# Keys of the cached sequences turned in place in three whole rooms, with the closing work of a sequence one period later and the sliding keys turned ahead of the scores

## The chip, the cores and the metric

The kernel runs on one core of one Trainium2 chip. The metric is the time of one execution on the device in microseconds (us), the median of several runs. Five engines work side by side, each through its own list of instructions in order: PE (TensorE: matmuls, and 128x128 transposes as matmuls with an identity), DVE (VectorE), ACT (ScalarE), POOL (GpSimd) and SP (SyncE, which here only issues transfers). POOL issues transfers too. An instruction that waits holds up all that stands behind it on its engine.

## The reference

The reference is one step of a one-layer decoder trunk. Two branches of attention are projected, merged by gates, and followed by an MLP. There are two groups of tokens: a prompt of 512 tokens, and a sample of 8 sequences with 8 new tokens each. Each sequence of the sample also has 2048 cached tokens, which lie in 16 pages of 128 tokens anywhere in a pool; a page table says where.

```
def fox_attend(q, cq, q_pos, k, v, ck, k_pos):
    s = jnp.einsum('btgrd,bsgd->bgrts', q, k).astype(jnp.float32) * HEAD_DIM ** -0.5
    bias = jnp.moveaxis(cq, 1, -1)[..., :, None] - jnp.moveaxis(ck, 1, -1)[..., None, :]
    p = masked_softmax(s + bias, k_pos[None, :] <= q_pos[:, None])
    return jnp.einsum('bgrts,bsgd->btgrd', p.astype(v.dtype), v)
...
    nsa_all = jnp.concatenate([gather_pages(nsa_pool, page_table), pm['nsa_rows']], axis=1)
    kc, vc, c_end = compressed_kv(nsa_all[:, :, 0], nsa_all[:, :, 1], lp)
...
    win_all = jnp.concatenate([win_buf, pm['win_rows']], axis=1)
...
    o_nsa = nsa_attend(pm['nsa_q'], pos[past:], pm['nsa_gate'], kc, vc, c_end, ks_blk, vs_blk,
                       win_all[:, :, 0], win_all[:, :, 1], w_pos)
```

For this case the attention of the sample over its cache matters. Each sequence has 64 rows of queries for the forgetting branch (8 heads by 8 tokens) and 64 for the sparse branch. Both meet all 2048 cached keys of the sequence (the sparse branch with a mask of chosen blocks added), a softmax follows, and the weights meet the 2048 cached values. The sparse branch has beside this a sliding window of 512 keys per sequence, and compressed keys, which an earlier stage has finished. All arithmetic here is in float32.

## The kernel before, in words

The stages are: conditioning and projections; attention of the prompt; attention of the sample (`sample_attention`); gates and branch projections (`mix_part`); output projection; MLP. A scheduler with a model of the engines sets the order inside most stages. Inside the sample's attention the order of PE's work is the one in which the code is written (`self.chain`).

**A sequence's data.** The cached rows of a sequence are 4.2 MB: 2 MB of the forgetting branch (`foxD`, gathered earlier into one place) and 2 MB of the sparse branch, page by page from `cache_nsa_kv`. They are loaded in four quarters (`sample_load`). A quarter is one transfer of 512 KB and four of 128 KB, one kind issued by SP and the other by POOL (line 155), by turns. The quarters go round a ring of ten places, called `r2`, `rp`, `L`, `s` and `U` in the code, with two quarters each; so two and a half sequences have room. In the trace the tiles are named `rows` (the places `r2` and `rp`), `fr` and `sr`. A row holds 128 numbers of keys and 128 of values.

**A sequence's period.** For sequence b the steps are:

1. `key_turn` (L1646): eight transposes on DVE in blocks of 32x32, from the quarters into two tiles `KT`. A ninth (L1650, `CT`) turns the bias terms, which POOL copies first (L1648).
2. `sequence_scores`: 64 matmuls `ss<-KT` and 8 `ss<-CT` on PE, each with 512 columns into a bank of its quarter. DVE adds a ramp and takes the maximum (L1671, `sS`), four times.
3. `new_scores` (`sn`, L1682): the scores against the new tokens.
4. `sequence_weights`: maximum over all (L1688, L1689 on DVE), then three exponentials on ACT.
5. `turn_weights`: 16 PE transposes `sp` and their eviction by ACT (`spT`), and one `spn` (`TN`).
6. `values(b)`: 128 + 4 matmuls `so<-rows`, `so<-fr`, `so<-sr`, `so<-vnew`. They are done one period later, behind the scores of b+1.
7. `sequence_end` (L1728 and on, `OA`) and `sums` (`accS`): scaling and the sum over heads, right behind `values`.

The window works for two sequences at once. On even b, behind the scores and values, come `window_keys` (`wk`, eight PE transposes), `window_scores` (`sw`, L1756) and `window_weights`. On odd b come `window_turned` (`spw`, `spwn`, evicted into `TW` by ACT and DVE) and `window_values` (`so<-wr`, `so<-vnew,TW`, `so<-vc`), then the loads of the next two windows (`wr`).

**The order of a period before.** Scores of b; new scores; weights of b; on odd b the window's values and loads; values of b-1; closing of b-1; the four quarters 4b+6 to 4b+9, that is the last two of b+1 and the first two of b+2; on even b the sums of two sequences; `key_turn` of b+1 (held back until the maximum of b is taken); on even b the window's keys, scores and weights; the turning of the weights of b. In the last period the first matmuls of the gates (`mix_first`, `mg<-hH`) stand ahead of the last `turn_weights`; their weights (`wmr`, `wmh`) are loaded from the last exponential on, and `hL` takes the place `r2` after the last values.

Helpers: L77 is every matmul, L83 every PE transpose, L112 every ACT operation, L115 a copy, L104 and L106 operations with a scalar, L155 a transfer.

## Time and profile before

| | |
|---|---|
| median of 3 runs | 1332.19 us (1330.32 to 1332.41) |
| the profiled execution, its own time | 1332.86 us |
| its span, first to last instruction | 1331.2 us |
| mean granted TensorE clock | 0.936 |
| PE busy | 1220.8 us (92%) |
| DVE busy | 689.3 us (52%) |
| ACT busy | 495.6 us (37%) |
| POOL busy | 179.6 us (13%) |

The last eviction of the prompt's attention starts at 465.6 us, the copies of the sample's result at 687.3 and 687.6 us; the sample's attention lies between. A line of the profile that groups instructions gives the engine, the operation, output and inputs by the program's names, shapes and count, then the busy time and the mean of one, then the idle time of the engine ahead of them and what ended it. A line of the waits gives the engine and the instruction that waited, what it waited for, then the total, the number of waits and the longest. A line of the windows gives a stretch of time, its length, the busy time of PE, of its weight loads, of DVE, ACT and POOL (with numbers of instructions), then the granted clock (1.00 is full speed), the DMA engines' mean busy share and the GB/s that they moved.

### The profile page before, as it was taken

The numbers are of one execution on the slowest core, as the hardware profiler recorded it, in microseconds if no ns is written. First come the engines' busy times: TensorE is split into PE (matmuls) and PEld (weight loads), VectorE is DVE, ScalarE is ACT, GpSimd is POOL, SyncE is SP. The second block draws the span as 40 slices with busy tenths as digits, with TensorE's granted clock in tenths as the row PEclk, the third lists the DMA queues.
The fourth block names the chain that finished last, engine by engine and source line by source line (L and its number), as shares of the span: only waits on it lengthen the run. The fifth ranks groups of instructions, "written<-read, shape, count | busy, mean of one in ns | idle before, by whom it ended". The sixth has DMA issues, their size and how long they took to land. (4 is left out here: it accounts for less than half of the span.)

```text
span 1331.2 us, 24902 instructions
## 1 busy us (share of the span) xinstructions
PE 1220.8 (92%) x9561; PEld 1018.3 (76%) x9561; DVE 689.3 (52%) x1820; ACT 495.6 (37%) x1082; POOL 179.6 (13%) x252
## 2 busy tenths in 40 slices
PE   4899989998999986687868999999999999999998
PEld 4777879996666533433468999999899898898996
DVE  4687756685788453433333434465334343343445
ACT  3444444445777621321332223346432142231321
POOL 2101000003213122312120000000111020111110
PEclk9899989999999966866678999999999999999999
DMA  8785266877756354654464333403342142232202
GB/s 229 227 252 163 91 206 205 268 259 229 246 180 189 112 183 162 227 184 159 135 161 141 85 82 103 127 1 96 95 127 67 60 121 70 64 95 83 76 17 71
DMA packets 164057, 188.11 MB, mean 141 GB/s; under 512 B 16186, under 2 KB 141571, under 8 KB 161763
## 3 DMA queue, kind: packets, MB, share of 16 engines
q1 hardware_dynamic: 145218, 146.15, 36.1%
q0 software_dynamic: 13408, 37.23, 8.6%
q10 hardware_dynamic: 5312, 3.15, 0.9%
q8 instruction: 75, 1.23, 0.4%
q14 instruction: 44, 0.35, 0.1%
HBM read 176.48 MB, written 30.90 MB: 156 GB/s over the span
## 5 line engine op out<-in xcount | busy, mean ns | idle before, releaser
L1984 POOL TENSOR_TENSOR u<-u 128x576 f32<-128x576 f32 x32 | 53.9, 1685 | 417.7 <-ACT u L112 327.7
L77 PE MATMUL mg<-hH,wmh 128*128 128x288 f32 x256 | 77.2, 303 | 7.2 <-ACT wmh L112 7.2
L77 PE MATMUL mg<-hL,wmh 128*128 128x288 f32 x256 | 74.8, 303 | 6.7 <-DMA hL<-hfd 6.7
L100 DVE TENSOR_TENSOR acc<-acc,dn 128x512 f32<-128x512 f32 x60 | 39.8, 686 | 77.4 <-PE dn L77 77.4
L77 PE MATMUL ss<-KT,scr 32*32 32x512 f32 x512 | 54.8, 932 | 26.6 <-DVE KT L1646 26.6
L77 PE MATMUL mg<-hH,wml 128*128 128x288 f32 x256 | 77.2, 303 | 0.7 <-DVE wml L131 0.7
L112 ACT ACTIVATE xh<-ct 128x256 fp32r<-128x256 f32 x128 | 48.0, 384 | 59.9 <-PE ct L83 38.4
L131 DVE TENSOR_TENSOR xl<-ct,xh 128x256 fp32r<-128x256 f32 x128 | 51.5, 421 | 17.6 <-ACT xh L112 15.8
L83 PE MATMUL ct<-identF,ro 128*128 128x128 f32 x256 | 37.7, 289 | 24.6 <-DVE ro L115 18.9
L763 DVE TENSOR_TENSOR u<-u,u 128x512 fp32r<-128x512 f32 x64 | 28.3, 484 | 61.3 <-ACT u L112 61.3
L131 DVE TENSOR_TENSOR wml<-wmr,wmh 128x1024 fp32r<-128x1024 f32 x16 | 19.6, 1225 | 76.3 <-ACT wmh L112 76.3
L77 PE MATMUL z<-winh,h2r 128*128 128x264 f32 (+1 forms) x288 | 57.1, 288 | 0.0
L77 PEld LDWEIGHTS ss<-KT,scr 32*32 32x32 f32 x512 | 12.5, 139 | 56.8 <-issue 47.7
L77 PE MATMUL z<-winh,h 128*128 128x264 f32 (+1 forms) x288 | 55.7, 283 | 0.0
L77 PEld LDWEIGHTS mg<-hH,wmh 128*128 128x128 f32 x256 | 49.9, 195 | 7.3 <-ACT wmh L112 7.3
L77 PEld LDWEIGHTS mg<-hL,wmh 128*128 128x128 f32 x256 | 48.1, 193 | 8.0 <-DMA hL<-hfd 8.0
L1671 DVE CUSTOM_DVE_ANT_1 sS<-ss,scr 128x512 f32<-128x512 f32 x32 | 20.8, 689 | 63.6 <-PE ss L77 63.6
L83 PEld LDWEIGHTS ct<-identF,ro 128*128 128x128 f32 x256 | 30.8, 150 | 28.1 <-DVE ro L115 17.5
L77 PEld LDWEIGHTS mg<-hH,wml 128*128 128x128 f32 x256 | 49.8, 195 | 1.0 <-DVE wml L131 1.0
L77 PEld LDWEIGHTS z<-winh,h2r 128*128 128x128 f32 x288 | 45.5, 189 | 1.2 <-issue 0.8
L77 PEld LDWEIGHTS z<-winh,h 128*128 128x128 f32 x288 | 45.7, 189 | 0.0
L112 ACT ACTIVATE u<-up 128x256 f32<-128x256 f32 (+1 forms) x96 | 27.8, 324 | 48.1 <-PE up L77 48.0
(849 smaller groups left out, 3670.3 us busy)
## 6 DMA issues: line engine op xcount, KB each, us to landing
adw<-in_w_ada SPq DMA_DIRECT2D x16, 1024.0 KB
foxD<-in_cache_fox_kv SPq DMA_DIRECT2D x128, 128.0 KB
wur<-in_w_up SPq DMA_DIRECT2D x32, 512.0 KB
wdr<-in_w_down SPq DMA_DIRECT2D x32, 512.0 KB
cpg<-in_cache_nsa_kv SPq DMA_DIRECT2D x120, 128.0 KB
wada<-in_w_ada POOLq DMA_DIRECT2D x8, 1024.0 KB, 6.9
wmr<-in_w_in SPq DMA_DIRECT2D x16, 512.0 KB
winr<-in_w_in SPq DMA_DIRECT2D x10, 512.0 KB
```

The source lines that it names most:

```text
L77: ins = self.nc.tensor.matmul(out, a, b, start=start, stop=stop, skip_group_check=True)
L83: ins = self.nc.tensor.transpose(out, in_, self.identF[:n, :n])
L100: self.nc.vector.tensor_tensor(out, a, b, op=op)
L112: return self.nc.scalar.activation(out, in_, f, **kw)
L131: self.splits.append((eng or self.nc.vector).tensor_tensor(l, x, h.bitcast(F32), op=OP.subtract).ins)
L763: (eng or self.nc.vector).tensor_tensor(h2[:, o:o + n], x[:, i:i + n], h2[:, i:i + n].bitcast(F32), op=OP.subtract)
L1671: self.nc.vector.tensor_tensor_reduce(self.S[:, :, q, :], pbs[q].rearrange("p (c s) -> p c s", s=32), self.ramp[:, None, 32 * (q % 2):32 * ...
L1984: nc.gpsimd.tensor_tensor(u[j], u[j], u[j], op=OP.mult)
```

## The change: three rooms, keys turned in place, another order of the period

**Rooms.** A sequence now has a room of its own for all 16 pages, and there are three: sequence b takes room b mod 3. Room 0 is made of the places `r2` (forgetting branch) and `rp` (sparse branch), rooms 1 and 2 lie in pools of their own. The load keeps its four quarters of transfers. Sequence 0 is loaded during the prompt's attention; 1 and 2 at the start of the sample's attention, behind the first two windows; b+2 in the period of b, behind the values of b-1, which free the room.

**Keys.** The eight transposes write back to where they read. The tiles `KT` are gone. The scores' matmuls read their 512 columns as 16 runs of 32 numbers, one run per page, 1 KB apart; before, the 512 numbers lay side by side.

**Order of a period.** On even b the window's keys come ahead of the scores, its scores behind the new scores, its weights behind the maximum. On odd b the window's turning and values (`window_back`) come ahead of the values of b-1. The closing of b-2 now stands in period b, behind the maximum; the sums come at the end of odd periods, one pair later. `key_turn` of b+1 follows the closing. The second part of `TW` is evicted by ACT.

**End.** In the last period the window's values, the values of sequence 6, the load of `hH` and the opening of the gates' weights come ahead of the last scores. The first gate matmuls stand between the last turning, values and closings.

The core of the diff:

```diff
             if n == 8:
                 self.forget_load(pn)
-                with self.tc.issue_after(self.last_min):
-                    for u in (2, 3):
-                        self.sample_load(u)
...
             if n == 9:
                 assert not (self.ada_open or self.ada_next)
-                for u in range(2):
-                    self.sample_load(u)
+                with self.tc.issue_after(self.last_min):
+                    self.sample_load(0)
...
-    RING = ("r2", "r2", "rp", "rp", "L", "L", "s", "s", "U", "U")
...
+        k = b % 3
+        if k == 0:
+            f = self.keep.tile([P, 16, 256], F32, tag="r2", bufs=1, name=f"fr{b}")
+            r = self.rp.tile([P, 16, 256], F32, tag="rp", name=f"sr{b}")
         else:
...
+            f, r = [self.spools[k].tile([P, 16, 256], F32, tag=n, bufs=1, name=f"{n}{b}") for n in ("fr", "sr")]
+        for i in range(4):
+            one, two = ("gpsimd", "sync") if i % 2 else ("sync", "gpsimd")
+            self.dma(two, f[:, 4 * i:4 * i + 4], self.foxD[b][:, 4 * i:4 * i + 4])
...
-        for u in range(4, 10):
-            self.sample_load(u)
-            if u == 5:
-                for b in range(2):
-                    self.window_load(b)
         self.key_turn(sp, 0)
+        for b in range(2):
+            self.window_load(b)
+        self.sample_load(1)
+        self.sample_load(2)
         self.sample_maps(sp)
...
+            if b == last:
+                self.window_back(pw, n)
                 self.values(b - 1)
...
+                self.hH = self.rp.tile([P, NK, NT], F32R, tag="rp", name="hH")
+                self.dma("gpsimd", self.hH, self.hfd[:, :, 0:NT])
+                ctx.close()
+                self.mix_open()
+            if not odd:
                 for o in range(2):
...
+                    self.window_keys(pw, b + o)
+            self.sequence_scores(sp, b)
+            self.new_scores(sp, b)
+            if not odd:
+                self.window_scores(pw, n)
+            self.sequence_max(b)
+            if not odd:
+                self.window_weights(n)
+            if b > 1:
+                self.sequence_end(sp, b - 2)
+                if not odd:
+                    self.window_end(sp, n - 1)
+            if b < last:
                 with self.tc.issue_after(self.last_stat):
                     self.key_turn(sp, b + 1)
-            if on and not odd:
+            if odd and b < last:
+                self.window_back(pw, n)
                 for o in range(2):
...
+                    self.window_load(b + 1 + o)
+            if 0 < b < last:
+                self.values(b - 1)
+                if b + 2 < NB:
+                    self.sample_load(b + 2)
+            self.turn_weights(sp, b)
+            if odd and b > 1:
+                self.pair_sums(n - 1)
+        self.mix_first(0)
+        self.values(last)
+        self.window_end(sp, 3)
+        for k in (1, 2):
+            self.mix_first(k)
+        for b in (last - 1, last):
+            self.sequence_end(sp, b)
+        self.mix_first(3)
+        self.pair_sums(3)
...
-        self.KT = [sp.tile([P, 4, 16, 32], F32, tag=f"KT{n}", bufs=1, name=f"KT{n}_{b}") for n in range(2)]
         for i in range(4):
-            for n, src in enumerate(self.rows[4 * b + i]):
-                self.nc.vector.transpose(self.KT[n][:, :, 4 * i:4 * i + 4, :].rearrange("p k c s -> p c k s"),
-                                         src[:, :, 0:P].rearrange("p c (k d) -> p c k d", k=4))
+            for src in self.rows[b]:
+                v = src[:, 4 * i:4 * i + 4, 0:P].rearrange("p c (k d) -> p c k d", k=4)
+                self.nc.vector.transpose(v, v)
...
-                                self.KT[x // 2][part[q], 2 * (x % 2) + e].rearrange("p c s -> p (c s)"), e == 0, False)
+                                self.rows[b][x // 2][part[q], :, 64 * (x % 2) + 32 * e:64 * (x % 2) + 32 * e + 32], e == 0, False)
...
-        self.cp(self.TW[:NS, 4], tn[:NS, 0:P])
+        self.act(self.TW[:NS, 4], tn[:NS, 0:P])
```

The scheduler places the transposes of sequence 0 on DVE. This is DVE's list before, in the last part of the prompt's attention (`Sfox` adds a bias to the prompt's scores and takes a maximum, `oT<-ofox` evicts an output):

```order
L104 TENSOR_SCALAR ncn<-cumn 64x64 [waits PE_49]
L115 COPY scr<-scr 64x8x8 [waits DVE_49]
L115 COPY scr<-scr 64x4x8 x2
L104 TENSOR_SCALAR scr<-scr 128x64 [waits DVE_49]
L100 TENSOR_TENSOR oT<-ofox_6095,Ffox_6069 128x512 [waits PE_49,Activation_49]
L100 TENSOR_TENSOR scr<-pers,scr 128x8x64 [waits DVE_49]
L1203 ISA Sfox_6181,nmfox_6182<-sfox_6203,browfox_5911 128x512 [waits PE_49]
```

And now, at the same place:

```order
L104 TENSOR_SCALAR ncn<-cumn 64x64 [waits PE_49]
L100 TENSOR_TENSOR scr<-pers,scr 128x8x64 [waits DVE_49]
L1652 STREAM_TRANSPOSE fr_6121<-fr_6121 128x4x128 [waits DMAHW4_49,DMASW0_49]
L1652 STREAM_TRANSPOSE sr_6122<-sr_6122 128x4x128 [waits DMAHW6_49,DMAHW7_49,DMAHW1_49,DMAHW0_49]
L100 TENSOR_TENSOR oT<-ofox_6065,Ffox_6039 128x512 [waits PE_49,Activation_49]
L1200 ISA Sfox_6182,nmfox_6183<-sfox_6221,browfox_5913 128x128 [waits PE_49]
L1200 ISA nmfox_6183 128x1
L1652 STREAM_TRANSPOSE fr_6121<-fr_6121 128x4x128 [waits DMAHW2_49]
```

The first transposes of the sample, each waiting for its transfers, now stand ahead of an output's eviction and of the maxima of the prompt's scores; before, the first of them stood behind the last `oT<-ofox`.

POOL's list at the start of the sample's attention, before (`jj` is a ramp of 64 numbers from which DVE makes the selectors `sel` and `selW`; an `ISA` computes a page's address):

```order
L1216 COPY ffox_6419<-denfox_6352 128x512
L155 DMA fr_6533<-foxD_80 128x1024
L162 TENSOR_LOAD ptp
L155 ISA
L155 DMA sr_6550<-in_cache_nsa_kv 128x256
...
L155 DMA wr_6565<-in_state_win_kv 128x1024
L155 DMA wr_6567<-in_state_win_kv 128x1024
L155 DMA fr_6569<-foxD_80 128x1024
L125 IOTA jj 128x64
```

And now:

```order
L1213 COPY ffox_6418<-denfox_6351 128x512
L155 DMA wr_6543<-in_state_win_kv 128x1024
L155 DMA wr_6545<-in_state_win_kv 128x1024
L155 DMA fr_6547<-foxD_80 128x1024
...
L155 DMA fr_6605<-foxD_81 128x1024
L162 TENSOR_LOAD ptp
L155 ISA
L155 DMA sr_6606<-in_cache_nsa_kv 128x256
...
L155 DMA sr_6606<-in_cache_nsa_kv 128x256
L125 IOTA jj 128x64
```

The ramp stood behind POOL's share of two quarters, both windows and one transfer more; now it stands behind both windows and POOL's whole share of sequences 1 and 2, 22 transfers. On DVE the first selector, which waits for the ramp, stood ahead of all four `sS` of sequence 0; now it stands between the second and the third.

ACT's list in an odd period, before (`sS` and `sN` are the exponentials of the sequence, `spT` evicts its turned weights):

```order
L112 ACTIVATE TW_7971<-spw_7964 128x512
L112 ACTIVATE sS_7949,ss_5_7947<-sS_7949,ss_5_7948 128x1024 x2
L112 ACTIVATE sN_7957,ss_5_7947<-sN_7957,ss_5_7948 128x64
L112 ACTIVATE spT_8161<-sp_8156 128x512
L112 ACTIVATE spT_8168<-sp_8163 128x512
```

And now:

```order
L112 ACTIVATE TW_7969<-spw_7962 128x512
L112 ACTIVATE sS_7931,ss_5_7929<-sS_7931,ss_5_7930 128x1024 x2
L112 ACTIVATE sN_7939,ss_5_7929<-sN_7939,ss_5_7930 128x64
L112 ACTIVATE TW_7969<-spwn_7963 64x128
L112 ACTIVATE spT_8131<-sp_8126 128x512
```

The eviction of `spwn`, for which PE's `so<-vnew,TW` waits, came from DVE; now it stands on ACT behind the three exponentials.

More of the change, by code (lines that the diff above doesn't have):

```diff
@@ L1406, in sample_select @@
         pb = self.accb("selx")
[L1407 removed]
+        sel2 = self.carve([P, 2, 32])
         nc.vector.memset(sel2, 0.0)
@@ L1571, in sample_attention @@
         self.key_turn(sp, 0)
+        for b in range(2):
+            self.window_load(b)
+        self.sample_load(1)
+        self.sample_load(2)
         self.sample_maps(sp)
-        for b in range(NB + 1):
-            n, odd, on = b // 2, b % 2, b < NB
-            if on:
-                self.sequence_scores(sp, b)
-                self.new_scores(sp, b)
-                self.sequence_weights(b)
-            if on and odd:
-                self.window_turned(pw, n)
-                self.window_values(sp, n)
-                if b + 2 < NB:
-                    for o in range(2):
-                        self.window_load(b + 1 + o)
-            if b:
-                self.values(b - 1)
-                self.sequence_end(sp, b - 1)
-                for u in range(4 * b + 6, min(4 * b + 10, 4 * NB)):
-                    self.sample_load(u)
-            if on and odd:
-                self.window_end(sp, n)
-            if b and not odd:
-                for o in range(2):
-                    self.sums(b - 2 + o, self.sel, self.OA[o], True)
-                    self.sums(b - 2 + o, self.selW[o], self.OAw, False)
-            if b + 1 < NB:
+        last = NB - 1
@@ new lines, in sample_attention @@
+        for b in range(NB):
+            n, odd = b // 2, b % 2
+            if b == last:
+                self.window_back(pw, n)
+                self.values(b - 1)
+                self.hH = self.rp.tile([P, NK, NT], F32R, tag="rp", name="hH")
[3 more added lines that the diff above has]
+            if not odd:
+                for o in range(2):
+                    self.window_keys(pw, b + o)
[11 more added lines that the diff above has]
+            if b < last:
@@ L1617, in sample_attention, with window_back, pair_sums @@
             self.cp(self.oT[:, 4 * a:4 * a + 4, SEQ:NT].rearrange("p r (b t) -> p r b t", t=8), av[:, a])
+    def window_back(self, pw, n):
+        self.window_turned(pw, n)
+        self.window_values(pw, n)
+    def pair_sums(self, n):
+        w = self.OAw.pop(n)
+        for o in range(2):
+            self.sums(2 * n + o, self.sel, self.OA.pop(2 * n + o), True)
+            self.sums(2 * n + o, self.selW[o], w, False)
     def sample_maps(self, sp):
@@ L2050, in run @@
         self.staged = 0
-        self.rows, self.wr, self.pair = {}, {}, {}
+        self.rows, self.wr, self.wst = {}, {}, {}
         actx = ExitStack()
```

71 lines of the change are left out of this document (23 added, 48 removed).

## The prediction

> **What bounds the kernel now.** I read the page first. PE is busy for 92% of the span; the rows of the forty slices (33.3 us each, tenths) tell where it is not, and where its clock is low:
>
> ```profile
> PE   4899989998999986687868999999999999999998
> PEclk9899989999999966866678999999999999999999
> ```
>
> Only slices 15 to 21 have both a PE below 9 and a clock down to 6: 466 to 699 us, the sample's attention. The windows give that stretch exactly, with the end of the prompt's attention ahead of it:
>
> ```profile
> core 0: us, PE busy (x) PEld busy (x) DVE busy (x) ACT busy (x) POOL busy (x), PEclk, DMA share, GB/s
> 440.00:460.00 20.00, 19.85 (x169) 11.83 (x169) 7.24 (x23) 13.61 (x37) 1.52 (x3) 1.00 0.17 51
> 466.35:687.60 221.25, 167.15 (x2208) 87.69 (x2208) 85.82 (x251) 51.55 (x111) 44.13 (x87) 0.68 0.50 167
> ```
>
> PE works 167.15 us of 221.25 and idles 54.1. DVE and ACT are busy for 86 and 52 us, and the transfers for half of it, so no engine is the bound; waits in a chain are. And the mean clock of 0.68 makes part of PE's work longer. The lines of the stretch, one tile after the other, price what PE waits for:
>
> ```profile
> L77 PE MATMUL ss<-KT,scr 32*32 32x512 f32 x512 | 54.8, 932 | 26.6 <-DVE KT L1646 26.6
> L77 PE MATMUL mg<-hH,wmh 128*128 128x288 f32 x18 | 6.5, 376 | 7.2 <-ACT wmh L112 7.2
> L77 PE MATMUL accS<-sel,OA 128*64 128x64 f32 x32 | 3.0, 270 | 6.8 <-DVE OA L106 6.7
> L83 PE MATMUL spn<-identF,sN 128*64 128x128 f32 x8 | 2.4, 298 | 6.5 <-DVE swst L1756 6.5
> ```
>
> These four hold 47.0 of the 54.1 us (the rest are gaps of a microsecond or two). The largest is the keys, and the waits say that the keys in turn wait for transfers, 35 us on DVE in the two largest rows:
>
> ```profile
> DVE KT L1646 <- DMA fr<-foxD: 19.6, 6, 6.8
> DVE KT L1646 <- DMA rows<-foxD: 15.3, 6, 4.3
> ```
>
> That is the ring of two and a half sequences: the last quarters of b+1 are asked for only when the values of b-1 are done. The clock shows in one matmul: 587 ns at its shortest, 1056 in the middle. The timeline has a sequence of each kind, sequence 1 from 492.76 to 498.63 and sequence 2 from 517.77 to 529.45:
>
> ```profile
> L77 PE MATMUL ss<-KT,scr x512: 587/1056/1058, 470.7 to 657.4; 32*32 32x512 f32 x171
> ...
> 470.67 4.23 PE L77 MATMUL ss<-KT,scr 32*32 32x512 f32 x32 [5.23 <-DVE KT L1646]
> ...
> 492.76 1.95 PE L77 MATMUL ss<-KT,scr 32*32 32x512 f32 x32
> 498.63 0.27 PE L77 MATMUL sn<-knT,bdF 128*64 128x64 f32 x1
> ...
> 517.77 4.14 PE L77 MATMUL ss<-KT,scr 32*32 32x512 f32 x32 [9.33 <-DVE KT L1646]
> 529.45 0.37 PE L77 MATMUL sn<-knT,bdF 128*64 128x64 f32 x1
> ```
>
> So scores take 5.87 us at full clock and 11.68 at half. Only sequences 1 and 3 have the short form in the timeline; six of eight are long, which costs 6 x 5.81 = 35 us.
>
> **The change part by part.** The sum is made against the profiled execution's own 1332.86 us, which is 0.7 above the median of the runs.
>
> *The keys' wait.* 26.6 us in all. The first wait, 5.2 us ahead of 470.67, is that of sequence 0 and is priced below. The other 21.4 come from quarters asked for in the period in which they are needed. Now they are asked for a whole period earlier. How long a sequence's load takes, the windows of the load issued at about 531 us show:
>
> ```profile
> 531.00:536.00 5.00, 2.79 (x112) 2.47 (x103) 3.51 (x10) 2.71 (x6) 3.54 (x8) 0.83 0.67 184
> ...
> 540.00:544.50 4.50, 4.50 (x22) 3.13 (x23) 1.40 (x4) 1.19 (x2) 0.00 (x0) 0.68 1.00 359
> 544.50:548.00 3.50, 3.50 (x47) 2.07 (x47) 1.14 (x8) 2.95 (x7) 0.00 (x0) 1.00 0.10 39
> ```
>
> The engines go quiet after 13.5 us for 4.2 MB. A period takes 27 us now (216.5 from the first scores to 687.2, by 8) and by this sum 21, so the last quarter lands 1 to 7 us before its turn. I take -21.4 us, and +3 for quarters that come late (bounds 0 and 12, 2 us in each of six periods).
>
> *The clock.* In the rows above the clock falls after a long idle stretch (9.33 us ahead of 517.77) and stays low through all 11.68 us of scores, though PE is then busy without a gap. It comes back under full-array work, transposes and values. So with fewer waits ahead of them, more scores run at full clock. What lies between two scores now:
>
> ```profile
> 503.18 3.01 PE L77 MATMUL so<-rows,spT 128*32 128x64 f32 x128
> 506.36 1.97 PE L83 MATMUL sp<-identF,sS 128*128 128x128 f32 x16
> ...
> L1646 DVE STREAM_TRANSPOSE KT<-fr 128x512 f32<-128x512 f32 x18 | 12.5, 693 | 19.6 <-DMA fr<-foxD 19.6
> L1650 DVE STREAM_TRANSPOSE CT<-scr 128x512 f32<-128x512 f32 x8 | 5.4, 669 | 0.0
> L1756 DVE CUSTOM_DVE_ANT_0 sW<-sw,scr 128x512 f32<-128x512 f32 x4 | 2.7, 672 | 1.6 <-PE sw L77 1.6
> ...
> L83 PE MATMUL wk<-identF,wr x32: 272/374/477, 482.9 to 641.4; 128*128 128x128 f32 x32
> ```
>
> Even sequences (2, 4, 6) follow closely on values, turning, sums and the window's keys, all full-array work: fast. Odd ones follow on a turning, and their key transposes stand on DVE behind the maximum: the window's 0.7, then 8 x 0.69 and 0.67, 6.9 us. PE meanwhile waits some 3 us for the exponentials (below), mostly under the values (3.01), and turns weights (1.97); it then idles 1.5 to 2 us. I expect sequences 0 and two of 3, 5, 7 slow: three instead of six, 3 x 5.81 = -17.4. Other work in cold stretches is longer too (`wk` above: 272 ns at its shortest, 477 at its longest); I put it at a fifth of the scores' part, an estimate without a row of its own: -3.5 (0 to -7).
>
> [...]
>
> *The other waits of PE.* The sums wait for `OA` (6.7) since the closing follows its values at once; now a period lies between. The last weight transposes wait for DVE's work on the window (`spn` 6.5); the window now lies earlier. The first gate matmuls wait 7.2 us for `wmh`, asked for at the last exponential; now at the one before, a period earlier. Together -20.4; nothing in the new order puts another wait there before the work of that period.
>
> *Added.* `so<-vnew,TW` now waits until ACT has done the exponentials:
>
> ```profile
> L112 ACT ACTIVATE sS<-sS,ss 128x1024 f32<-128x1024 f32 x16 | 18.2, 1140 | 60.9 <-DVE ss L1689 60.9
> L112 ACT ACTIVATE sN<-sN,ss 128x64 f32<-128x64 f32 x8 | 2.7, 333 | 0.0
> 502.60 0.44 PE L77 MATMUL so<-vnew,TW 64*32 64x64 f32 x8 [1.47 <-DVE TW L115]
> ```
>
> Two of 1.14 and one of 0.33, with short reads of the sums between them, are some 3 us; PE has a little work meanwhile and waits 1.5 already: +2.3 in sequences 1, 3 and 5, +7 (bounds 0 and 10). Behind it stand the values of b-1, and behind them the load of b+2. The wait for key transposes ahead of odd sequences: 3 x 2 = +6 (0 to 12).
>
> *Sequence 0.* Its transposes, in the prompt's attention now, save the 5.2 us of PE ahead of its scores, which then end near 478 if still slow. But the ramp `jj` is issued behind 22 transfers. Each POOL transfer waited for an earlier one to land:
>
> ```profile
> 433.35 0.60 POOL L155 DMA_DIRECT2D rows<-foxD  x1 [1.93 <-DVE scr L100]
> ...
> 468.68 0.21 POOL L125 IOTA jj<- 128x64 f32 x1
> ...
> 478.69 1.13 POOL L155 DMA_DIRECT2D sr<-in_cache_nsa_kv  x2 [1.12 <-DMA fr<-foxD]
> ...
> rows<-foxD POOLq DMA_DIRECT2D x6, 512.0 KB, 5.9
> ```
>
> POOL ended its old list there, 17 transfers, at 479.8; with 22 it ends near 485, and only then come the last two `sS` of sequence 0. So the 5.2 us are given back: 0 (-5 to +5).
>
> *The prompt.* DVE reaches the first transposes at about 437.2, by these rows; the transfers, issued from 433.35 on with 5.9 us to landing, are there at 439 to 440:
>
> ```profile
> 436.03 0.68 DVE L100 TENSOR_TENSOR scr<-pers,scr 128x512 f32<-128x512 f32 x1
> 436.63 0.68 DVE L1203 CUSTOM_DVE_ANT_0 Sfox<-sfox,browfox 128x512 f32<-128x512 f32 x1
> ```
>
> For 2 to 3 us DVE stands, and with it `oT<-ofox` and the prompt's maxima, while PE is 99% busy (19.85 of 20 us) and so has no slack to lose: +3 (0 to 6).
>
> *In-place turning and reading in runs.* The transposes read the same patterns and write as many numbers, eight per sequence before and after: 0. The matmuls read 16 runs of 128 bytes, 1 KB apart. The nearest rows are matmuls of 256 columns, the first of which reads runs of 128 bytes 256 bytes apart, the second a tile without gaps:
>
> ```profile
> L77 PE MATMUL qt<-bdF,identF x32: 379/379/403, 449.3 to 452.2; 128*32 128x256 f32 x32
> ...
> L77 PE MATMUL ada<-adw 128*32 128x256 f32 x256 | 17.1, 385 | 0.1
> ```
>
> 379 against 385 ns: I take 0; the upper bound is twice the time per sequence, a rival below, and nothing lets it gain.
>
> *After the stretch.* The gate matmuls wait for `hL`, whose place `r2` came free with the last values:
>
> ```profile
> 686.92 0.29 PE L77 MATMUL accS<-selW,OAw 128*64 128x64 f32 x4
> 689.44 0.66 PE L77 MATMUL mg<-hL,wmh 128*128 128x288 f32 x2 [2.23 <-DMA hL<-hfd]
> L77 PE MATMUL mg<-hL,wmh 128*128 128x288 f32 x256 | 74.8, 303 | 6.7 <-DMA hL<-hfd 6.7
> ```
>
> 6.7 us in all. `r2` now holds sequence 6, whose values come a whole period earlier: -4.5 (0 to -6.7).
>
> The sum: -21.4 + 3 - 17.4 - 3.5 - 20.4 + 7 + 6 + 0 + 3 + 0 - 4.5 = -48.2. 1332.86 - 48.2 = 1284.7; less 0.7 for the median, 1284 us.
>
> **The rivals.**
>
> *The clock stays high.* If the 1.5 to 2 us ahead of odd sequences do not bring the clock down, two more sequences are fast (-11.6) and the waits of +13 shrink by half: 1284 - 18 = 1266. For it: sequence 1 followed a warm turning at once and stayed at 587 ns. Against it: the two waits of `spn`, 6.5 us in all, each stood just ahead of a slow sequence. Chance 0.17.
>
> *The clock still falls each period, or the loads are still late.* With shorter periods the loads are 1 to 7 us early; if a period takes 17, they are late, PE waits for keys and starts cold as before. Then the 20.9 us of the clock are lost and 7 us of waits added: 1284 + 28 = 1312. This is also the case in which the change does not do what it says, the loads being asked for early and landing no sooner. Chance 0.20.
>
> *Slower: the runs of 128 bytes.* If a matmul that reads 16 runs 1 KB apart pays for each run, all 512 of them grow. The gain of 48 us is used up by 6 us in each of eight sequences, about twice the 5.87 us at full clock. With the three slow sequences doubled as well the price is 3 x 11.7 + 5 x 5.9 = 65 us, and the time 1349. For it: no row shows a step of 1 KB. Against: `qt` pays nothing for a step of 256 bytes. Chance 0.09.
>
> **How the numbers follow.** The forecast itself has 0.54. The range of 8 in 10 takes in both rivals that are faster than before, with their ends widened by the bounds of the late quarters and the prompt: 1260 to 1314. About 0.2% is what a measurement of this kernel can tell from no change, 2.7 us. Slower by more than that is the third rival at its full price, 0.09; within it, the third rival at about 1.7 times or the second with every bound at its end, 0.03; faster 0.88.
>
> **What would show it.** In the changed kernel's profile: `ss` waiting for key transposes under 10 us in all, and these for DMA near 0; the shortest `ss` matmul still 587 ns and its middle value below 1056; starts of scores about 21 us apart, 15 after even ones and up to 25 after odd; the sample's result copied near 640 us; no waits of `accS` for `OA` and of `mg` for `wmh`; a new wait of 2 to 3 us of `so<-vnew` for ACT; `jj` near 485 us. It would be wrong if the shortest `ss` matmul grew, if the first transposes held the prompt up by more than 6 us, or if the transfers took the keys' place as the last wait.

## The result, and the profile after

The changed kernel takes 1261.82 us in the median of 4 runs (1256.25 to 1262.31), against 1332.3 us (4 runs) before: a ratio of 0.9463, 95% interval 0.9434 to 0.9492. It is 70.5 us faster. The forecast was 48 us (1284, in a range of 1260 to 1314), so the time lies 1.8 us inside the fast end of the range; nearest to it is the first rival (the clock stays high, 1266 us). The profiled execution took 1261.79 us, its span is 1260.1 us, its mean clock 0.971. The ratios below leave out one run, the sixth of experiment 9, which took 2878 us, more than twice the usual time.

These are the two rows of slices of the page after, PE's busy share and its granted clock. A slice is now 31.5 us, and the sample's attention lies in slices 16 to 20:

```profile
PE   3789989999999988888899999999999999999998
PEclk9989999999999986888999999999999999999999
```

One slice has a clock of 6, where five had. Two stretches show where the time came from, first before, then after: from the first scores to the copies of the result, and the 81 matmuls behind the copies (each line: stretch, span, PE busy, ..., clock, DMA share, GB/s):

```profile
470.67:687.30 216.63, 167.15 (x2208) 87.69 (x2208) 81.20 (x244) 51.25 (x111) 40.15 (x78) 0.68 0.49 165
687.30:710.00 22.70, 16.04 (x81) 14.88 (x82) 10.12 (x15) 9.05 (x16) 7.58 (x15) 0.78 0.89 250
```

```profile
479.68:629.00 149.32, 127.82 (x2201) 74.22 (x2201) 76.82 (x228) 50.76 (x114) 49.28 (x95) 0.85 0.80 261
629.00:639.70 10.70, 10.70 (x81) 10.70 (x82) 9.58 (x14) 8.97 (x16) 0.00 (x0) 1.00 0.49 150
```

The stretch is 67.3 us shorter. PE's busy time fell by 39.3 us, because the clock rose from 0.68 to 0.85 for the same work (but for eight key transposes of the first window, some 2 us, which now lie ahead of the first scores), and its idle time fell from 49.5 to 21.5 us. The score matmuls show the clock directly; their middle value is now the shortest one, where before it was 1056 ns:

```profile
L77 PE MATMUL ss<-fr,scr x256: 584/587/1057, 479.7 to 611.4; 32*32 32x512 f32 x128
L77 PE MATMUL ss<-sr,scr x256: 584/587/1057, 479.9 to 611.4; 32*32 32x512 f32 x128
```

What PE waits for in the stretch, from the lines after (busy, mean ns, then idle and its cause):

```profile
L77 PE MATMUL ss<-fr,scr 32*32 32x512 f32 x256 | 34.1, 651 | 2.4 <-ACT spT L112 2.1 <-issue 0.3
L83 PE MATMUL sp<-identF,sS 128*128 128x128 f32 x128 | 20.4, 327 | 4.2 <-ACT sS L112 4.2
L77 PE MATMUL so<-vnew,TW 64*32 64x64 f32 x32 | 1.6, 291 | 7.4 <-ACT TW L112 7.4
```

No wait of `ss` for the transfers of keys, of `accS` for `OA`, of `spn` for the window or of `mg` for its weights is left. The largest wait is one that the prediction added, `so<-vnew` for the eviction on ACT. The 2.1 us of `ss` that the row puts down to `spT` are the other one, the key transposes ahead of odd sequences (see the point-by-point section).

Not all was gained. The prompt's attention ends later. Its first and its last evictions, before:

```profile
L100 DVE TENSOR_TENSOR oT<-oslc,Fslc x4: 653/689/692, 336.3 to 402.2; 128x512 f32<-128x512 f32 x4
L100 DVE TENSOR_TENSOR oT<-ofox,Ffox x4: 691/692/692, 435.4 to 465.6; 128x512 f32<-128x512 f32 x4
```

and after, with the waits of DVE and PE between them:

```profile
L100 DVE TENSOR_TENSOR oT<-oslc,Fslc x4: 651/687/692, 339.7 to 405.5; 128x512 f32<-128x512 f32 x4
L100 DVE TENSOR_TENSOR oT<-ofox,Ffox x4: 653/692/692, 445.8 to 475.4; 128x512 f32<-128x512 f32 x4
...
437.61 0.63 POOL L155 DMA_DIRECT2D fr<-foxD  x1 [2.44 <-PE cumn L77]
...
444.62 0.71 DVE L1652 STREAM_TRANSPOSE fr<-fr 128x512 f32<-128x512 f32 x1 [3.81 <-DMA fr<-foxD]
...
447.78 1.54 PE L83 MATMUL ptfox<-identF,Sfox 128*128 128x128 f32 x6 [4.89 <-ACT PTfox L112]
...
450.88 0.71 DVE L1652 STREAM_TRANSPOSE sr<-sr 128x512 f32<-128x512 f32 x1 [1.87 <-DMA sr<-in_cache_nsa_kv]
```

POOL's transfers of sequence 0 are issued from 437.61 us on; DVE stands 3.81 and 1.87 us at them, and PE 4.89 us behind it. The part between the two evictions grew from 129.3 to 135.7 us. While PE waited the clock fell too (0.66 between 443 and 453 us). The 3.4 us by which it begins later are taken as no effect of the change (last section).

The pieces add up: +3.4 ahead of it, +6.4 in the prompt, -0.8 from there to the first scores, -67.3, and -12.7 behind the copies make -71.0, and 1261.79 - 1332.86 is -71.07.

### The profile page after: what moved, and what is told of

It is laid out like the page before. It is cut to its first block, busy times and chain, and to the rows that moved or that the text cites. A ratio compares the mean times of both kernels' runs of the same rounds, so it can differ in the third digit from the quotient of the medians.

```text
span 1260.1 us, 24957 instructions
## 1 busy us (share of the span) xinstructions
PE 1178.5 (94%) x9561; PEld 1001.4 (79%) x9561; DVE 684.7 (54%) x1816; ACT 495.8 (39%) x1086; POOL 179.6 (14%) x252
## 3 DMA queue, kind: packets, MB, share of 16 engines
q8 instruction: 75, 1.23, 0.4%
## 4 chain that ended last, share of the span: by engine, by line
PE 84%; DVE 7%; DMA 4%; ACT 3%; issue 1%; SPq 0%; ACTq 0%; POOL 0%; DVEq 0%; POOLq 0%
PE dn L77 17%; PE up L77 16%; PE mg L77 8%; PE z L77 7%; PE hid L77 6%; PE wo L77 4%; PE br L77 4%; PE ss L77 4%; PE ct L83 2%; PE so L77 2%; PE ada L77 1%; DMA cpg<-in_cache_nsa_kv 1%; PE sp L83 1%; DMA sr<-in_cache_nsa_kv 1%; PE sfox L77 1%
## 5 line engine op out<-in xcount | busy, mean ns | idle before, releaser
L83 PE MATMUL ct<-identF,ro 128*128 128x128 f32 x256 | 37.6, 288 | 25.9 <-DVE ro L115 20.4
L131 DVE TENSOR_TENSOR xl<-ct,xh 128x256 fp32r<-128x256 f32 x128 | 51.4, 419 | 17.4 <-ACT xh L112 15.3
L77 PE MATMUL hid<-xh,w1hlk 128*128 128x512 f32 (+1 forms) x160 | 45.0, 369 | 0.1
L77 PE MATMUL hid<-xh,w1hlv 128*128 128x512 f32 (+1 forms) x160 | 44.0, 361 | 1.1 <-ACT xh L112 0.5
L77 PE MATMUL z<-winl,h2r 128*128 128x264 f32 (+1 forms) x160 | 44.5, 284 | 0.5 <-DVE winl L131 0.5
```

What stands on the lines that cost most here:

```text
L77: ins = self.nc.tensor.matmul(out, a, b, start=start, stop=stop, skip_group_check=True)
L83: ins = self.nc.tensor.transpose(out, in_, self.identF[:n, :n])
L131: self.splits.append((eng or self.nc.vector).tensor_tensor(l, x, h.bitcast(F32), op=OP.subtract).ins)
```

## Experiments

The theory after the result is that the rooms take the transfers out of the chain of scores, values, load, keys; with that PE no longer stands idle ahead of the scores, and the clock follows. The rival is that the new order of the window's and the closing work does it, and the early loads are a detail. The medians of before were 1331.2 us beside experiments 1 and 4 to 6, 1332.4 beside 2, 3, 7 and 8, and 1331.0 beside 9 to 12. Starts and lengths of the scores below are read from each timeline, of one execution per kernel. A sequence of 6 to 7 us has its scores at full clock, one of 11 to 14 at half (in the profile of before the granted clock is 1.00 in the window of sequence 1, 492.76 to 498.63 us, and 0.50 in that of sequence 0, 470.67 to 482.50), one between changed on the way. In "rooms alone" and "window behind" four score matmuls of sequence 0 run 4 us ahead of the start given.

| kernel | median us | scores: start (length), sequences 0 to 7 | PE waits named below |
|---|---|---|---|
| before | 1332.3 | 471 (11.8), 493 (5.9), 518 (11.7), 546 (6.1), 567 (11.7), 593 (12.2), 623 (11.7), 649 (11.3) | keys 26.6 |
| after | 1261.8 | 480 (11.5), 501 (6.7), 521 (6.3), 534 (6.7), 554 (6.2), 568 (6.7), 588 (6.3), 607 (6.5) | `so<-vnew` 7.4 |
| order alone | 1337.3 | 485 (11.3), 504 (11.7), 534 (11.7), 562 (11.7), 591 (11.7), 618 (11.7), 646 (12.6), 675 (11.3) | keys 29.9 |
| rooms alone | 1294.1 | 469 (12.4), 497 (13.6), 521 (6.5), 545 (7.2), 562 (6.5), 585 (7.2), 603 (6.4), 624 (6.4) | `accS` 16.7 |
| window behind | 1280.4 | 469 (13.5), 499 (13.6), 524 (6.6), 541 (11.9), 565 (6.5), 581 (8.3), 602 (6.4), 624 (6.3) | `spn` 8.3 |
| closing at once | 1276.4 | 476 (11.3), 498 (12.0), 523 (6.3), 543 (6.4), 562 (6.3), 581 (6.0), 599 (6.3), 623 (6.3) | `accS` 13.0 |
| TW on DVE | 1271.6 | 473 (11.3), 494 (12.0), 521 (6.1), 534 (10.4), 561 (6.0), 574 (6.7), 596 (6.0), 614 (6.3) | `so<-vnew` 13.6 |
| turned before | 1253.6 | 476 (11.5), 499 (6.7), 513 (6.4), 528 (7.0), 544 (6.3), 558 (6.8), 573 (6.5), 593 (6.5) | none of these |

**1. Loads at the old times.** The edit issues half of a sequence at a time:

```diff
                 self.values(b - 1)
+                self.sample_load(b + 1, 1)
                 if b + 2 < NB:
-                    self.sample_load(b + 2)
+                    self.sample_load(b + 2, 0)
+            if b < last:
+                with self.tc.issue_after(stat):
+                    self.key_turn(sp, b + 1)
```

> The three rooms, the keys turned in place and the new order of work stay; only the loads go back to the old calendar: behind the values of b-1 the second half of b+1 and the first half of b+2, and the key transposes of b+1 behind them. Theory (no idle stretch ahead of the scores, so the clock stays full): the keys' waits of about 21 us come back and at least four of the seven scores now fast fall to half clock at 5.8 us each, 1262 + 21 + 23 to 29 = 1306 to 1312 us, and the middle ss matmul is near 1056 ns again. Rival (the new order of window and closing work keeps the clock, the loads only remove waits): at most 1283 us, ss still at 587 ns.

Measured: 1261.66 us, ratio 0.9496 (0.9444 to 0.9547), all scores but the first fast. By its number that is the rival's case, but it settles nothing, because the edit did not do what it was meant to do. In the changed kernel POOL waits for the values of b-1 ahead of the load; in this one the first load goes out ahead of those values:

```profile
510.05 1.08 POOL L155 DMA_DIRECT2D wr<-in_state_win_kv  x2 [7.98 <-PE so L77]
517.56 0.53 POOL L155 DMA_DIRECT2D fr<-foxD  x1 [2.64 <-PE so L77]
```

```profile
503.54 1.08 POOL L155 DMA_DIRECT2D wr<-in_state_win_kv  x2 [7.98 <-PE so L77]
504.62 0.53 POOL L155 DMA_DIRECT2D fr<-foxD  x1
```

The second half of b+1 goes into a room that has been free for a period, so nothing holds it, wherever it stands in the code. What it does show is that half of the keys may be asked for about a period later at no cost: DVE then stands 15.6 us for their transfers, and PE hardly waits longer. The old times come from the places that are shared, so the ring itself had to come back.

**2. Order alone.** The rooms, loads and `KT` of before under the order of after:

```diff
+    RING = ("r2", "r2", "rp", "rp", "L", "L", "s", "s", "U", "U")
...
                 self.values(b - 1)
-                if b + 2 < NB:
-                    self.sample_load(b + 2)
+                for u in range(4 * b + 6, min(4 * b + 10, 4 * NB)):
+                    self.sample_load(u)
+            if b < last:
+                with self.tc.issue_after(stat):
+                    self.key_turn(sp, b + 1)
```

> The order of the changed kernel on the rooms of before: ring of ten quarters, loads behind the values of b-1, keys turned into KT. Theory (the rooms matter: a quarter's place comes free only with the values of b-1, so the last keys of b+1 land 6 to 8 us behind them): the keys' waits of 21 us come back, and four or five scores fall to half clock at 5.8 us each, 1262 + 21 + 23 to 29 = 1306 to 1312 us. Rival (the order alone carries the gain): at most 1275 us.

**3. Rooms alone.** Three rooms, early loads and turning in place under the order of before:

```diff
                 self.values(b - 1)
                 self.sequence_end(sp, b - 1)
-                for u in range(4 * b + 6, min(4 * b + 10, 4 * NB)):
-                    self.sample_load(u)
+                if b + 2 < NB:
+                    self.sample_load(b + 2)
+                if b == NB - 1:
+                    self.hH = self.rp.tile([P, NK, NT], F32R, tag="rp", name="hH")
+                    self.dma("gpsimd", self.hH, self.hfd[:, :, 0:NT])
...
-                for k in range(4):
-                    self.mix_first(k)
             if on:
                 self.turn_weights(sp, b)
+        for k in range(4):
+            self.mix_first(k)
```

> The three rooms, the loads a period ahead and the keys turned in place, in the order of before; only the end differs, where hH is loaded behind the values of sequence 6 and the first gate matmuls stand behind the last turning. Theory (the keys' waits of 21 us are the rooms' part, the other waits of 20 us and most of the half clock the order's): 1332 - 21 - 6 to 18 = 1293 to 1305 us. Rival (order carries all): 1315 us or more. Rival (rooms carry all): 1275 us or less.

Measured: the order alone takes 1337.29 us, ratio 1.0042 (1.0014 to 1.0070), 0.4% slower than before. Both expectations missed, and the theory's by 25 us: it left the order some gain of its own. The rooms alone take 1294.07 us, ratio 0.9710 (0.9691 to 0.9729), in the interval of the theory. So the rooms, with their early loads and the turning in place, which were not tried apart, give 38 us, the order alone nothing, and the order on top of the rooms another 32. The lines of the order alone tell why it gives nothing, together with one turn of its loop in the timelines:

```profile
L77 PE MATMUL ss<-KT,scr 32*32 32x512 f32 x512 | 62.3, 1056 | 29.9 <-DVE KT L1664 29.9
L1664 DVE STREAM_TRANSPOSE KT<-rows 128x512 f32<-128x512 f32 x20 | 13.2, 692 | 17.6 <-DMA rows<-foxD 15.8 <-DMA rows<-in_cache_nsa_kv 1.8
L1664 DVE STREAM_TRANSPOSE KT<-fr 128x512 f32<-128x512 f32 x18 | 12.5, 693 | 21.2 <-DMA fr<-foxD 21.2
...
549.25 0.55 POOL L155 DMA_DIRECT2D fr<-foxD  x1 [17.89 <-PE so L77]
...
561.16 0.71 DVE L1664 STREAM_TRANSPOSE KT<-fr 128x512 f32<-128x512 f32 x1 [1.52 <-DMA fr<-foxD]
...
562.01 3.63 PE L77 MATMUL ss<-KT,scr 32*32 32x512 f32 x28 [9.22 <-DVE KT L1664]
```

The values free the place at 549.25, the last quarter is turned at 561.16, the scores begin at 562.01 after 9.22 us of idle PE, at half clock (mean 1056 ns, all eight sequences). The period is scores at half clock, values, load, turning, and the work that was moved out of PE's way is not in it. PE only arrives earlier at the same keys, waits longer, and no sequence is fast any more. With the rooms alone the loop is open, and what remains are the waits that the new order takes away:

```profile
L77 PE MATMUL ss<-fr,scr 32*32 32x512 f32 x252 | 37.2, 652 | 0.0
L77 PE MATMUL accS<-sel,OA 128*64 128x64 f32 x32 | 3.3, 294 | 16.7 <-DVE OA L106 16.6
L83 PE MATMUL spn<-identF,sN 128*64 128x128 f32 x8 | 2.4, 294 | 5.7 <-DVE swst L1746 5.3 <-ACT spT L112 0.4
```

No wait for keys stands in the row of the scores, and six sequences are fast already. But the 5.3 us of `spn` stand ahead of sequence 1, where DVE's work on the window stood behind key transposes that waited for transfers (4.71 and 1.60 us), so the first loads are still felt there. `mg<-hH` waits 8.0 us for its load, at the end that this run has of its own. The sums' wait, 6.7 us before, has grown to 16.7; probably part of it had been hidden under the waits for keys.

**4 to 6. One part of the order undone at a time.** The window's keys, scores and weights behind the values again:

```diff
-            if not odd:
-                for o in range(2):
-                    self.window_keys(pw, b + o)
             self.sequence_scores(sp, b)
...
+            if not odd:
+                for o in range(2):
+                    self.window_keys(pw, b + o)
+                self.window_scores(pw, n)
+                self.window_weights(n)
             self.turn_weights(sp, b)
```

> Only the window's keys, scores and weights go back behind the values on even sequences. Theory: the two waits of spn for DVE return (6.5 us), and a gap of 3 us ahead of odd scores brings two or three of them to half clock, 1262 + 6.5 + 12 to 17 = 1280 to 1286 us. Rival (the clock hangs on the key waits alone): 1262 to 1269 us, with all scores but those of sequence 0 at 587 ns.

The closing right behind the values again:

```diff
                 self.values(b - 1)
+                self.sequence_end(sp, b - 1)
                 if b + 2 < NB:
                     self.sample_load(b + 2)
+                if odd:
+                    self.window_end(sp, n)
+                else:
+                    self.pair_sums(n - 1)
```

> Only the closing goes back: sequence_end right behind the values, the sums of a pair in the next even period. Theory of the prediction: the sums wait for OA again, 6.7 us, 1268 to 1270 us. Rival: 5.5 of these 6.7 us were OA standing on DVE behind key transposes that waited for transfers; with the keys early it costs nothing, 1261 to 1264 us.

The second part of `TW` on DVE again:

```diff
-        self.act(self.TW[:NS, 4], tn[:NS, 0:P])
+        self.cp(self.TW[:NS, 4], tn[:NS, 0:P])
```

> Only the second part of TW is evicted by DVE again, ahead of or among the key transposes, not by ACT behind the exponentials. Theory: the wait of so<-vnew,TW (7.4 us in the changed kernel) shrinks to about 3, 1257 to 1259 us; if this gap is also what brings the clock down in three odd periods, values and turning there run at full clock and the time is 1248 to 1253 us. Rival: DVE is in the key transposes at that time, so TW comes as late, 1260 to 1264 us.

Measured: 1280.40 us (ratio 0.9610, 0.9570 to 0.9649), 1276.43 us (0.9595, 0.9560 to 0.9630) and 1271.61 us (0.9568, 0.9533 to 0.9603). The row of each that came back, window, closing and `TW` in this order:

```profile
L83 PE MATMUL spn<-identF,sN 128*64 128x128 f32 x8 | 2.5, 316 | 8.3 <-DVE swst L1760 7.4 <-ACT spT L112 0.8
```

```profile
L77 PE MATMUL accS<-sel,OA 128*64 128x64 f32 x32 | 3.0, 279 | 13.0 <-DVE OA L106 13.0
```

```profile
L77 PE MATMUL so<-vnew,TW 64*32 64x64 f32 x32 | 1.6, 290 | 13.6 <-DVE sd L1734 13.5
```

The window behind the values costs 19 us: 8.3 of waiting and three odd sequences at or partly at half clock (1, 3, 5 in the table). That is the theory's number, but not quite its cause. 7.4 us of the wait stand at one place, ahead of sequence 1, where DVE's work on the window stood behind key transposes that waited for transfers:

```profile
493.86 0.71 DVE L1650 STREAM_TRANSPOSE sr<-sr 128x512 f32<-128x512 f32 x1 [3.62 <-DMA sr<-in_cache_nsa_kv]
```

So here the window's place lets a wait for keys through to PE; that waits of the window without it would bring the clock down is not shown. The closing at once costs 15, and its wait in the trace is 13.0; the rival (it only waited behind transfers) fell, since DVE's key transposes alone hold `OA` up, and none of them waits for a transfer. For `TW` both expectations fell: on DVE it waits behind the key transposes for longer (13.6 us) than on ACT behind the exponentials (7.4), and the kernel is 10 us slower. Moving it to ACT was a gain of the change where the prediction had booked a cost against an unchanged DVE. In the traces of the closing and of `TW` sequence 1 is at half clock too (12.0 us), ahead of the first work that either edit moves, so these 5 us of each trace are not the edit's.

**7. Keys of sequence 0 behind the prompt.**

```diff
-        self.key_turn(sp, 0)
+        with self.tc.issue_after(self.last_min):
+            self.key_turn(sp, 0)
```

> Only the key transposes of sequence 0 are held back behind the last maximum of the prompt. Theory: the prompt's last eviction comes 6 us earlier, since DVE waits for no transfer ahead of its maxima, 1255 to 1257 us. Rival: the scores of sequence 0 wait for the first windows and for the ramp in any case, 1260 to 1263 us.

Measured: 1255.69 us, ratio 0.9427 (0.9410 to 0.9445). The prompt's price is shown: 6 us by the medians, and the part between its two evictions is 130.5 us again instead of 135.7. The scores of sequence 0 are fast now (6.1 us from 471.2 on), and what waits next is the ramp:

```profile
484.63 0.32 DVE L106 TENSOR_SCALAR sel<-jj,map,map 128x64 f32<-128x64 f32 x1 [8.90 <-POOL jj L125]
```

**8. The window's weights turned ahead of the maximum.**

```diff
+            if odd and b < last:
+                self.window_turned(pw, n)
             self.sequence_max(b)
...
-                self.window_back(pw, n)
+                self.window_values(pw, n)
```

> Only the window's turning is written ahead of the maximum on odd sequences, so that ACT evicts the second part of TW behind the first exponential, not behind all three. Theory: the wait of so<-vnew,TW falls from 7.4 to about 3 us, 1256 to 1258 us; if the clock then stays full through the values, 1248 to 1253 us. Rival: the exponentials come later by as much and the turning with them, 1260 to 1263 us.

Measured: 1261.74 us, ratio 0.9467 (0.9437 to 0.9496), no difference, though the wait of `so<-vnew,TW` fell to 2.2 us. The even sequences follow about 3 us sooner on 1 and 5 (16.4 and 17.7 us against 19.9 and 20.4), but sequence 3 fell to half clock in the trace (11.2 us), behind a wait of 1.94 us for its key transposes, and took it back. By the time alone the rival is not excluded.

**9. Ramp ahead of the loads**, on top of 7:

```diff
             self.window_load(b)
+        self.sample_maps(sp)
         self.sample_load(1)
         self.sample_load(2)
-        self.sample_maps(sp)
```

> The kernel with the transposes of sequence 0 held back (1255.7 us), and the ramp jj issued ahead of the loads of sequences 1 and 2. Theory: DVE's wait of 8.9 us for the ramp goes, and what ends next is the landing of sequence 1, some 17 us after its first issue, so 3 to 6 us are won: 1250 to 1253 us. Rival: the keys of sequence 1 land no earlier than the ramp did, 1255 to 1257 us.

Measured: 1256.17 us in the median of the five runs that the ratio takes (1257.93 with the one of 2878 us), ratio 0.9431 (0.9392 to 0.9470), the same as without it. By its number that is the rival, but not by its cause: sequence 1 began 16.1 us behind sequence 0 instead of 22.0. It ran at half clock (12.0 us), and so did most of sequence 5 (10.6 us): in the trace the gain went into the clock.

**10. Work that nobody uses**, on the changed kernel:

```diff
         for j in range(4):
             self.quarters(col, self.TW[:, j], [w[:, j, P:256] for w in wr], j == 0, False)
+        if i < 3:
+            fb = self.mmb(f"fill{i}")
+            for j in range(16):
+                self.tr(fb[:, P * (j % 4):P * (j % 4) + P], self.identF)
```

> The changed kernel with work added that nobody uses: 16 PE transposes of the identity, 2.1 us at full clock, in the wait of so<-vnew,TW in sequences 1, 3 and 5. Theory (full-array work decides the clock): the clock stays full in these periods, values and turning get faster by 2 to 3 us each, and the time falls to 1253 to 1257 us though 6.4 us of work are added; all so matmuls near 222 ns. Rival (the clock there falls for another reason): 1262 to 1266 us.

Measured: 1261.40 us, ratio 0.9489 (0.9449 to 0.9528), no difference in all and in neither interval, and the trace has sequence 1 at half clock (12.0 us; 6.7 in the changed kernel's). That arose ahead of any added work: PE stood 2.57 and 1.17 us at `swn` and `sp` of sequence 0. Whether the medians are equal for this reason is not shown. In the place itself the trace bears part of the theory out: with the wait filled, the clock there is 1.00 instead of 0.75. That it takes full-array work to keep it is not shown. From the window's turning in period 3 to the scores of sequence 4, in the changed kernel and then in this one:

```profile
541.00:554.40 13.40, 10.26 (x237) 8.76 (x233) 8.32 (x22) 6.01 (x14) 4.55 (x9) 0.75 0.71 244
```

```profile
538.80:549.70 10.90, 9.65 (x254) 8.26 (x253) 8.28 (x22) 6.04 (x14) 2.38 (x5) 1.00 0.79 265
...
540.96 1.97 PE L83 MATMUL fill<-identF 128*128 128x128 f32 x16
543.49 0.32 PE L77 MATMUL so<-vnew,TW 64*32 64x64 f32 x8 [0.56 <-ACT TW L112]
```

With 16 matmuls more, the same work ends 2.5 us sooner, at full clock; on sequence 5 the next one follows in 18.0 us instead of 20.4. Without the added 1.97 us the work takes PE 7.68 us instead of 10.26: the waits of 0.69 and 2.45 us had cost another 2.6 us by the clock.

**11. The window's weights turned ahead of the odd scores**, on the changed kernel:

```diff
+            if odd and b < last:
+                self.window_turned(pw, n)
             self.sequence_scores(sp, b)
...
-                self.window_back(pw, n)
+                self.window_values(pw, n)
```

> The changed kernel with only the window's turned weights (spw, spwn and their evictions) moved ahead of the odd scores. Theory: the wait of 7.4 us goes and nothing is left between the scores and the values but 1 us, so the clock stays full there: 1250 to 1255 us. Rival: the odd scores start later by the turning and its evictions, the time is 1260 to 1264 us.

**12. All three**: 7, 9 and 11 together.

> Transposes of sequence 0 held back, ramp ahead of the loads, window's turned weights ahead of the odd scores. If the three add up: 1241 to 1247 us. If the loads become the bound of the period: 1248 us or more.

Measured: 1253.55 us, ratio 0.9426 (0.9389 to 0.9462), in the theory's interval, and 1247.48 us, ratio 0.9371 (0.9335 to 0.9407), between the two. In 11 the wait is gone (scores of 3 to scores of 4 take 16.3 us against 20.3). With the wait gone in 11, or filled in 10, the clock stays full from sequence 1 (in 10, from its values) to sequence 7; in the changed kernel it does not. The lines are the changed kernel's, 11's and 10's:

```profile
500.63:606.00 105.37, 90.25 (x1784) 53.30 (x1788) 60.95 (x176) 39.11 (x89) 31.88 (x62) 0.90 0.73 245
498.50:602.50 104.00, 91.03 (x1875) 48.55 (x1875) 63.89 (x188) 39.69 (x90) 36.98 (x71) 1.00 0.84 276
512.20:607.70 95.50, 86.33 (x1798) 49.06 (x1797) 54.50 (x161) 35.16 (x79) 35.72 (x68) 1.00 0.89 287
```

The last kernel is the fastest of all, 14 us ahead of the changed one. The parts as measured (6, 0 and 8 us) add up to that; 3 to 6 us for the ramp, as expected for 9, never came, and in the last trace sequences 0 and 1 are still slow.

## Why the prediction came out as it did, point by point

**The keys' wait (-21.4, and +3 for late quarters): right.** No wait of `ss` for transfers of keys is left. Experiments 2 and 3 show that it was the shared places, not the order; the turning in place came with the rooms.

**The other waits of PE (-20.4) and the added ones (+13): right in the sum, not in each part.** PE's idle time in the stretch was forecast to fall by 25.8 us (the five terms of the stretch that are waits) and fell by 28.0. `so<-vnew` waits 7.4 us where 7 were added. But this was no cost of the move to ACT; on DVE, with the keys early, it would be 13.6 (experiment 6). The wait for key transposes ahead of odd sequences, +6, is there at sequences 3 and 5 alone, with 0.90 and 1.23 us. The row names ACT, but the last transpose of `fr` on DVE ends at 534.01 us, just ahead of the scores, where the eviction that the row takes had ended 0.41 us earlier; in experiment 10 the same wait is put down to DVE:

```profile
534.10 1.06 PE L77 MATMUL ss<-fr,scr 32*32 32x512 f32 x8 [0.90 <-ACT spT L112]
533.34 0.67 DVE L1652 STREAM_TRANSPOSE fr<-fr 128x512 f32<-128x512 f32 x1
...
531.93 1.06 PE L77 MATMUL ss<-fr,scr 32*32 32x512 f32 x8 [1.23 <-DVE fr L1652]
```

So the path was right and the wait shorter than the 1.5 to 2 us of the prediction: PE needs the transposes of `fr` first, and those of `sr` and `CT` run on beside its first scores.

**The clock (-20.9): the direction right, the size wrong.** This is the step that failed, and it failed in two terms. PE's busy time fell by 39.3 us instead of 20.9. The scores' part (-17.4) came to 25.6 (the lengths in the table add up to some 82.5 us before and 56.9 after): "I expect sequences 0 and two of 3, 5, 7 slow" rested on 1.5 to 2 us of idle PE; with 0.90 and 1.23 us the clock held in this trace, and only sequence 0 was slow. The other work in cold stretches (-3.5, "an estimate without a row of its own", 0 to -7) came to 13.7, some 2 of it work that now lies ahead of the stretch. So about half of the 18.4 us that were missed lie in a term that was hardly priced; the window's scores, for one, went from 9.1 to 5.0 us of busy PE.

The first rival, with a chance of 0.17, was what happened by its outcome. Its condition, that 1.5 to 2 us of waiting do not bring the clock down, is not shown: in experiment 8 the wait ahead of sequence 3 is 1.94 us, and that sequence is slow. The margin is thin. In experiment 9 the wait ahead of sequence 5 is 1.23 us, as long as in the changed kernel, and there the scores take 10.6 us instead of 6.7; what decides between the two is open. That waits of PE bring the clock down, and are not only found beside it, is shown by experiments 10 and 11 for the wait of `so<-vnew` (in period 3, from the window's turning to the scores of sequence 4, the changed kernel has a clock of 0.75 and experiment 10, with the wait filled, 1.00; experiment 11, without the wait, has 1.00 in the line above); for the waits ahead of the scores it is argued from experiments 2 to 6.

How long the clock stays down differs in the runs. At sequence 0 of the changed kernel it is at half through all 11.5 us of scores, and in the order alone through all eight, 11.3 to 12.6 us each. In period 3 of the changed kernel it fell when 1.9 us of the waits of 0.69 and 2.45 had passed, with small matmuls between them, and came back 6.82 us later, 5.59 of which PE was busy, in the turning of the weights behind the values:

```profile
541.08:544.49 3.41, 1.49 (x39) 0.97 (x37) 3.34 (x12) 2.29 (x4) 0.93 (x2) 1.00 0.92 328
544.49:551.31 6.82, 5.59 (x157) 5.08 (x158) 4.02 (x9) 1.18 (x5) 0.96 (x3) 0.50 0.53 191
551.31:552.00 0.69, 0.69 (x9) 0.69 (x7) 0.00 (x0) 0.55 (x2) 0.43 (x1) 1.00 1.16 273
```

What sets the moment of the fall and of the return is not shown.

**The prompt (+3): too small.** It cost 6.4 us in the trace and 6.1 by experiment 7. The step counted from the first issue of before, 433.35 us, had the transfers land at 439 to 440, and DVE stand 2 to 3 us once. POOL issued them from 437.61 on (3.4 of these 4.3 us are the later begin), DVE stood 3.81 us, until 444.62, and 1.87 us more at the second quarter. A fall of the clock behind PE's wait of 4.89 us was not in the sum.

**Sequence 0 (0): right.** Not each POOL transfer of before had waited for an earlier one: six waits of this kind, of 0.3 to 2.3 us, stand from 470.5 us on, none ahead of them. The ramp came at 491.8 us, DVE waited 5.2 us for it, and the scores of sequence 0 were slow.

**Behind the copies (-4.5): too small.** All 6.7 us of `hL` went. The clock, for which the sum had no term here, rose from 0.78 to 1.00, and the 81 matmuls behind the copies took 10.70 us of busy PE instead of 16.04, which is 5.3 us. Of the 12.7 us measured 0.7 stay without a name.

**Runs of 128 bytes, 1 KB apart (0): right.** The shortest and the middle score matmul are 584 and 587 ns; with side-by-side columns the shortest was 587.

In the profiled execution the forecast fell 22.9 us short. The clock in the stretch is 18.4 of it, the part behind the copies 8.2, the idle time 2.2 and the start of the scores 0.8; the prompt (3.4) and its later begin (3.4) take 6.8 back. So it is in part luck that the time lies inside the range: without the prompt's extra 3.4 us alone the median would be 1258.4 us.

## What to carry to other kernels

Look for the closed loop first: where a buffer's reader releases the load of what the next round needs, a rearrangement of other work need not shorten the round (here it gave nothing), and the same rearrangement can be worth a lot once the loop is open (here 32 us). Where the trace shows the clock lower behind a wait, count the wait at more than its length: add what the work behind it loses (here the waits of 0.69 and 2.45 us cost another 2.6, experiment 10), and say at which idle time you think that the clock falls, because a forecast turns on it. Price the clock for all work of the stretch, with a row for each part, and not only for the largest. A step that only moves to another engine is to be priced against the queue of the old engine as it will be after the change, not as it is before.

## What the runs showed of the hardware that was not expected

With work that nobody uses the clock stayed full: 16 transposes, in the place of a wait of 2.45 us, kept it at 1.00 where it was 0.75, and the same work of period 3 ended 2.5 us sooner (experiment 10).

The time of the same code varies by several us ahead of everything that the change touches. Before 80 us the kernels are alike, and yet PE's longest wait there, for the first normalised rows, is 5.06 us in the profile of before and 9.13 us in that of after:

```profile
60.99 1.97 PE L83 MATMUL nt<-identF,x 128*128 128x128 f32 x8 [5.06 <-DVE x L104]
```

```profile
66.94 1.97 PE L83 MATMUL nt<-identF,x 128*128 128x128 f32 x8 [9.13 <-DVE x L104]
```

In the fourteen traces here the prompt's first eviction starts between 332.2 and 342.9 us. So differences under some 5 us between two kernels were read from the stretch in question, not from the whole time. Why this wait varies was not tried.
